# Scale and shift of a modulated norm as columns on transposed rows, and a pool of their own for the head norms

## The chip, the cores and the metric

The kernel runs on one core of one Trainium2 chip. The metric is the device time of one execution in microseconds (us); several runs of each kernel are taken on the same chip, and their medians are compared. A core has five engines that work side by side, each through a queue of its own in a fixed order: PE (TensorE, the matrix multiplier; PEld is its weight load), DVE (VectorE), ACT (ScalarE), POOL (GpSimd) and SP (SyncE, which here issues the DMA transfers).

## The reference

The program runs two transformer blocks over 512 tokens of width 2048. The first block (sparse attention and a state-space mixer) ends in a projection and a layernorm. The second block is a modulated one; this is its beginning, where the change sits:

```python
def rms_norm(x, g):
    xf = x.astype(jnp.float32)
    y = xf * lax.rsqrt(jnp.mean(xf * xf, axis=-1, keepdims=True) + EPS)
    return (y * g.astype(jnp.float32)).astype(x.dtype)
...
        sub = jnp.einsum('bse,ed->bsd', mixed, w_out[layer])
        h = _layer_norm(DEEPNORM_ALPHA * h + sub, ln_g[layer], ln_b[layer])
...
    mod_shared = jax.nn.silu(c) @ w_mod + b_mod
        mod = (mod_shared + mod_layer[l])[:, None, :]
        shift1, scale1, gate1, shift2, scale2, gate2 = jnp.split(mod, N_MOD, axis=-1)
        h = rms_norm(x, norm1_g[l]) * (1.0 + scale1) + shift1
        proj = h @ w_in[l]
        u_a, v_a, q, k, v = jnp.split(proj, SPLIT_POINTS, axis=-1)
        y_a = chunked_spatial_gating(u_a, v_a, gm_norm_g[l], gm_ws[l], gm_bs[l])
        q = rms_norm(q.reshape(B, S, N_SB_HEADS, HEAD_DIM), q_norm_g[l])
        k = rms_norm(k.reshape(B, S, N_SB_HEADS, HEAD_DIM), k_norm_g[l])
```

Behind it come stick-breaking attention, an output projection, a second modulated norm and a mixture of 32 experts of which each token uses two.

## The kernel before, in words

The 512 tokens lie in four tiles of 128, called rows 0 to 3 here (one token on each partition, 2048 values along it). For a matmul the rows must be transposed, so that the 2048 features stand on partitions, 16 blocks of 128.

All large products are exact to fp32 by splitting: each operand becomes a high part, cast to the matmul's fp32r type on ACT (L123, `split_into`), and a low part, the rest, subtracted on DVE (L124); `mm3` (L148 to L150) multiplies high by high, high by low and low by high. Weights stream in chunks: SP loads 512 KB into `raw` (4 buffers, L136), ACT casts it into `wh`, DVE subtracts `wl` (3 buffers each), PE multiplies. With two rows of tokens a chunk is 12 matmuls of 128x512.

`phase_b` computes the w_out product for rows 0 and 1, then for rows 2 and 3, in 4 column blocks of 8 chunks each. Behind each block DVE adds the residual (L761) and gathers statistics (L762); behind each pair of rows `norms` runs for each of the two. It applies the layernorm (L780, L781, into `r`), stores the row (L782), squares it on ACT (L783), gets the reciprocal root from small DVE operations (L192 to L197), and then for each quarter of 512 features multiplies on DVE (L788) and adds on GpSimd (L789):

```python
            nc.vector.scalar_tensor_tensor(t[:, c], r[:, i, c], rs, g1[:, c], OP.mult, OP.mult)
            nc.gpsimd.tensor_tensor(t[:, c], t[:, c], s1[:, c], OP.add)
            self.rows_to_op(t[:, c], self.opt[2 * b:2 * b + 2], i)
```

`rows_to_op` transposes four blocks into a PSUM tile `s` on PE (L203) and splits them into `op` from there (L123, L124). Here g1 is norm1_g times (1 + scale1) and s1 is shift1, each one value for a feature, so each is loaded broadcast over all 128 partitions: 128x2048, 1 MB. `load(k)` spreads these loads over the first blocks.

`mixer2` then multiplies the normed rows by w_in: q for rows 0 and 1, k for rows 0 and 1, q for rows 2 and 3, k for rows 2 and 3, 8 chunks each. Each result gets a norm by heads of 128 (`head_norm`: four squares on ACT at L798, DVE's reciprocal root, L803 writes `row`), four transposes of `row` and a copy (L835).

The order on each engine is fixed when the program is built: a scheduler places the instructions of all engines by modelled times and data dependences, so code that is written later can stand between earlier code's instructions, and matmuls of q's and k's chunks between transposes. Tiles come from pools; a pool on the right side of the memory (`side='right'`) lies where an earlier one lay, and its tiles wait for the old tiles' last readers. `ln` holds lng, lnb, g1, s1 and the work tiles of the norm; `b2`, with gq, gk, go, gm, ws and the head norms' tiles, comes after it in the same place. `issue_after` asks the scheduler to put an instruction behind a named one.

Of the kernel before, what the change touches and what calls it, by code (L numbers as in the profile page):

```python
# [12 lines left out]
F32 = mybir.dt.float32  # L13
# [3 lines left out]
AF = mybir.ActivationFunctionType  # L17
OP = mybir.AluOpType
# [5 lines left out]
KT = 16  # L24
# [79 lines left out]
class Kern:  # L104
# [622 lines left out]
    def phase_b(self):  # L727
        tc, nc, a = self.tc, self.nc, self.a
        kw = dict(bufs=1, side='right', reuse_waits='tile')
        r = self.r = self.rr.tile([128, 4, 2048], F32, name='r')  # L730
        self.x1 = self.dram.tile([512, 2048], F32, name='x1')
        with tc.tile_pool(name='ln', **kw) as ln:
            t = [ln.tile([128, 2048], F32, name=n) for n in ('lng', 'lnb', 'g1', 's1')]
            lng, lnb, g1, s1 = t
            st = ln.tile([128, 4, 4, 6], F32, name='st')

            def load(k):

# [12 lines left out]

            for half in ((0, 1), (2, 3)):
                for b in range(4):
                    ps = self.gemm('R', a['w_out'][b], self.opm, bg=1, toks=half)
                    if half[0] == 0:
                        with tc.issue_after(self.last_load.ins):
                            load(2 * b)
                            load(2 * b + 1)
                    for i in half:
                        c = slice(b * 512, b * 512 + 512)  # L760
                        nc.vector.scalar_tensor_tensor(r[:, i, c], r[:, i, c], ALPHA, ps[i], OP.mult, OP.add)  # L761
                        nc.vector.bn_stats(st[:, i, b, :], r[:, i, c])  # L762
                for i in half:
                    self.norms(ln, i, st[:, i], lng, lnb, g1, s1)
        with tc.tile_pool(name='rt', **kw) as self.rt:
            with tc.tile_pool(name='b2', **kw) as b2:
                self.mixer2(b2, self.opt)
            with tc.tile_pool(name='m0', **kw) as self.m0:
                self.route()

    def norms(self, ln, i, st, lng, lnb, g1, s1):

        nc, r = self.nc, self.r
        mv = ln.tile([128, 2], F32, tag='mv', name='mv', bufs=2)
        nc.vector.bn_aggr(mv, st.rearrange('p b s -> p (b s)'))
        nc.vector.tensor_scalar(mv[:, 1:2], mv[:, 1:2], 1e-5, None, OP.add)
        rs = self.rsqrt(mv[:, 1:2], 1)
        t = ln.tile([128, 2048], F32, tag='t', name='t', bufs=2)
        ss = ln.tile([128, 4], F32, tag='ss', name='ss', bufs=2)
        nc.vector.scalar_tensor_tensor(t, r[:, i, :], mv[:, 0:1], lng, OP.subtract, OP.mult)  # L780
        nc.vector.scalar_tensor_tensor(r[:, i, :], t, rs, lnb, OP.mult, OP.add)  # L781
        nc.sync.dma_start(self.x1[i * 128:(i + 1) * 128, :], r[:, i, :])  # L782
        nc.scalar.activation(t, r[:, i, :], AF.Square, accum_out=ss[:, 0:1])  # L783
        nc.vector.tensor_scalar(ss[:, 0:1], ss[:, 0:1], 1.0 / 2048, 1e-6, OP.mult, OP.add)
        rs = self.rsqrt(ss[:, 0:1], 1)
        for b in range(4):
            c = slice(b * 512, b * 512 + 512)
            nc.vector.scalar_tensor_tensor(t[:, c], r[:, i, c], rs, g1[:, c], OP.mult, OP.mult)  # L788
            nc.gpsimd.tensor_tensor(t[:, c], t[:, c], s1[:, c], OP.add)  # L789
            self.rows_to_op(t[:, c], self.opt[2 * b:2 * b + 2], i)  # L790

    def head_norm(self, pool, x, g, out, scale=1.0 / 128, eps=1e-6):

        nc = self.nc
# [5 lines left out]
        rs = self.rsqrt(ss, 4)  # L800
        for h in range(4):
            c = slice(h * 128, h * 128 + 128)
            nc.vector.scalar_tensor_tensor(out[:, c], x[:, c], rs[:, h:h + 1], g[h], OP.mult, OP.mult)  # L803

    def mixer2(self, b2, op):
        tc, nc, a, r = self.tc, self.nc, self.a, self.r
        kw = dict(bufs=1, side='right', reuse_waits='tile')
        gq = self.row_bcast(b2, a['q_norm_g'], 128, 'gq')
        gk = self.row_bcast(b2, a['k_norm_g'], 128, 'gk')
        bs = b2.tile([128, 4], F32, name='bs')  # L810
        nc.sync.dma_start(bs, a['gm_bs'])
        one = b2.tile([128, 128], F32R, name='one')
# [13 lines left out]
        with tc.tile_pool(name='sb', **kw) as sb:  # L826
            for b, g, half in ((0, gq, (0, 1)), (1, gk, (0, 1)), (0, gq, (2, 3)), (1, gk, (2, 3))):
                ps = self.gemm('R', a['w_in_2'][b], op, bg=1, toks=half)
                xT = qk[b]
                for i in half:  # L830
                    t = b2.tile([128, 512], F32, tag='row', name='row', bufs=3)
                    self.head_norm(b2, ps[i], [g] * 4, t)
                    pt = self.sps()
                    self.transposes(pt, [t[:, h * 128:(h + 1) * 128] for h in range(4)])
                    nc.scalar.copy(xT[:, :, i * 128:(i + 1) * 128], pt.rearrange('p (h t) -> p h t', h=4))  # L835
# [15 lines left out]
            for b in range(4):  # L851
                nc.sync.dma_start(self.gate1[b], self.mod[:, 4096 + b * 512:4608 + b * 512].broadcast_to([128, 512]))

            nc.vector.tensor_tensor(ws, ws, self.mask_le[:, None, :].to_broadcast([128, 4, 128]), OP.mult)
            ps = self.gemm('R', a['w_in_2'][3], op)
            for i in range(4):
                t = b2.tile([128, 512], F32, tag='row', name='row', bufs=3)
                vn = b2.tile([128, 512], F32, tag='row', name='vn', bufs=3)
                nc.scalar.activation(t, ps[i], AF.Gelu)
                self.head_norm(b2, t, [gm[:, h * 128:(h + 1) * 128] for h in range(4)], vn)  # L860
# [8 lines left out]
            ps.update(self.gemm('R', a['w_in_2'][4], op, toks=(2, 3)))  # L869
            opy = [self.op_tiles(c) for c in range(4)]  # L870
            for i in range(4):
                t = b2.tile([128, 512], F32, tag='row', name='row', bufs=3)
                self.head_norm(b2, o[:, i, :], [go[:, 512 + h * 128:512 + (h + 1) * 128] for h in range(4)], t)
                self.rows_to_op(t, opy[0:2], i)
            for i in range(4):
                t = b2.tile([128, 512], F32, tag='row', name='row', bufs=3)
                vn = b2.tile([128, 512], F32, tag='row', name='vn', bufs=3)
                nc.scalar.activation(t, ps[i], AF.Gelu)  # L878
                nc.vector.tensor_tensor(t, t, sg[:, i, :], OP.mult)
                self.head_norm(b2, t, [go[:, h * 128:(h + 1) * 128] for h in range(4)], vn)  # L880
                self.rows_to_op(vn, opy[2:4], i)
        self.opy = opy

# [568 lines left out]
```

## Time and profile before

| | before |
|---|---|
| median of 3 runs | 2021.39 us (2020.11 to 2024.66) |
| the profiled execution | 2020.36 us, its span 2018.5 us |
| mean granted TensorE clock | 0.973 of full speed |
| PE / DVE / ACT / POOL busy | 95% / 60% / 43% / 16% of the span |
| DMA | 502.85 MB, mean 249 GB/s |

The span is the time from the first to the last instruction in the profile of one execution; the 1.9 us beside it are start and end of the program. Busy shares are means over stages of very different character, so a single stage has to be read from the time windows. An instruction's waiting time is shown in brackets with what released it.

### The profile page before, as it was taken

The numbers are of one execution on the slowest core, as the hardware profiler recorded it, in microseconds if no ns is written. First come the engines' busy times: TensorE is split into PE (matmuls) and PEld (weight loads), VectorE is DVE, ScalarE is ACT, GpSimd is POOL, SyncE is SP. The second block draws the span as 40 slices with busy tenths as digits, with TensorE's granted clock in tenths as the row PEclk, the third lists the DMA queues.
The fourth block names the chain that finished last, engine by engine and source line by source line (L and its number), as shares of the span: only waits on it lengthen the run. The fifth ranks groups of instructions, "written<-read, shape, count | busy, mean of one in ns | idle before, by whom it ended". The sixth has DMA issues, their size and how long they took to land. (4 is left out here: it accounts for less than half of the span.)

```text
span 2018.5 us, 30419 instructions
## 1 busy us (share of the span) xinstructions
PE 1909.2 (95%) x11830; PEld 1232.9 (61%) x11830; DVE 1217.5 (60%) x2210; ACT 862.8 (43%) x1426; POOL 325.9 (16%) x251
## 2 busy tenths in 40 slices
PE   8999999999999999999997999889589999999996
PEld 5677776666777778887876888778442333333331
DVE  4778975444677796558796664877633434333433
ACT  3343223335443453434444554644234444444453
POOL 0422133000011110001111120043331111111111
PEclk9999999999999999999998999989699999999998
DMA  8654664545665674586654332656699999999994
GB/s 305 224 188 166 232 230 169 181 179 204 239 218 199 213 258 136 183 311 235 197 200 144 116 116 96 248 199 219 260 346 358 399 400 399 401 403 396 401 416 183
DMA packets 115493, 502.85 MB, mean 249 GB/s; under 512 B 22299, under 2 KB 23835, under 8 KB 84499
## 3 DMA queue, kind: packets, MB, share of 16 engines
q1 hardware_dynamic: 108642, 479.81, 64.0%
q0 software_dynamic: 6080, 16.83, 3.2%
q10 hardware_dynamic: 624, 4.24, 0.5%
q8 instruction: 94, 1.54, 0.3%
q14 instruction: 53, 0.43, 0.1%
HBM read 479.76 MB, written 37.84 MB: 256 GB/s over the span
## 5 line engine op out<-in xcount | busy, mean ns | idle before, releaser
L124 DVE TENSOR_TENSOR wl<-raw,wh 128x1024 fp32r<-128x1024 f32 (+1 forms) x272 | 357.8, 1320 | 224.4 <-ACT wh L123 223.5
L123 ACT CAST wh<-raw 128x1024 fp32r<-128x1024 f32 (+1 forms) x272 | 280.5, 1031 | 445.9 <-PE g L150 200.7
L149 PE MATMUL g<-wl,op 128*128 128x512 f32 (+1 forms) x896 | 351.0, 392 | 5.6 <-DVE wl L124 5.5
L150 PE MATMUL g<-wh,op 128*128 128x512 f32 (+1 forms) x896 | 348.3, 389 | 0.0
L148 PE MATMUL g<-wh,op 128*128 128x512 f32 (+1 forms) x896 | 333.7, 393 | 2.1 <-ACT row L878 1.0
L148 PE MATMUL g<-op,wh 128*128 128x512 f32 x672 | 272.0, 406 | 4.4 <-ACT z L404 3.0
L149 PE MATMUL g<-op,wh 128*128 128x512 f32 x672 | 268.1, 400 | 0.0
L150 PE MATMUL g<-op,wl 128*128 128x512 f32 x672 | 262.2, 396 | 0.0
L1178 PE MATMUL s<-wop,x 128*32 128x512 f32 x1710 | 251.4, 593 | 0.0
L1180 PE MATMUL s<-wop,x 128*32 128x512 f32 x570 | 251.0, 593 | 0.0
L148 PEld LDWEIGHTS g<-wh,op 128*128 128x128 f32 x896 | 171.2, 191 | 42.8 <-issue 6.6
L149 PEld LDWEIGHTS g<-wl,op 128*128 128x128 f32 x896 | 171.0, 191 | 41.6 <-DVE wl L124 8.5
L150 PEld LDWEIGHTS g<-wh,op 128*128 128x128 f32 x896 | 170.8, 191 | 33.4 <-issue 1.1
L1178 PEld LDWEIGHTS s<-wop,x 128*32 128x32 f32 x1710 | 68.2, 110 | 158.2 <-issue 154.0
L148 PEld LDWEIGHTS g<-op,wh 128*128 128x128 f32 x672 | 127.6, 190 | 52.9 <-issue 19.7
L150 PEld LDWEIGHTS g<-op,wl 128*128 128x128 f32 x672 | 127.3, 189 | 31.6 <-issue 3.9
L1188 ACT COPY yt<-g 32x512 f32<-32x512 f32 x192 | 111.3, 580 | 79.4 <-DVE y L1271 43.2
L149 PEld LDWEIGHTS g<-op,wh 128*128 128x128 f32 x672 | 127.9, 190 | 26.2 <-issue 1.4
L1178 PE MATMUL g<-wop,hT 128*32 128x512 f32 x810 | 120.7, 592 | 3.7 <-ACT hT L1227 2.2
L1189 DVE TENSOR_TENSOR gu<-gu,s 96x512 f32<-96x512 f32 x32 | 21.8, 682 | 169.5 <-ACT gu L1188 169.5
L1188 ACT COPY gu<-s 32x512 f32<-32x512 f32 x96 | 55.6, 579 | 159.1 <-PE s L1180 157.5
L1180 PE MATMUL g<-wop,hT 128*32 128x512 f32 x270 | 120.9, 594 | 0.0
(400 smaller groups left out, 2817.9 us busy)
## 6 DMA issues: line engine op xcount, KB each, us to landing
wop<-in_w_gu SPq DMA_DIRECT2D x95, 1024.0 KB
raw<-in_w_in SPq DMA_DIRECT2D x168, 512.0 KB
wm<-in_w_mod SPq DMA_DIRECT2D x96, 512.0 KB
raw<-in_w_mod SPq DMA_DIRECT2D x96, 512.0 KB
raw<-in_w_out SPq DMA_DIRECT2D x96, 512.0 KB
wop<-in_w_dn SPq DMA_DIRECT2D x45, 1024.0 KB
w<-in_w_gu SPq DMA_DIRECT2D x33, 1024.0 KB
w<-in_w_dn SPq DMA_DIRECT2D x19, 1024.0 KB
```

The lines of the kernel that those rows point to most:

```text
L123: nc.scalar.copy(hi, src)
L124: (lo_eng or nc.vector).tensor_tensor(lo, src, hi.bitcast(F32), OP.subtract)
L148: nc.tensor.matmul(out, lhsT=a[0], rhs=b[0], start=start, stop=False)
L149: nc.tensor.matmul(out, lhsT=a[0], rhs=b[1], start=False, stop=False)
L150: nc.tensor.matmul(out, lhsT=a[1], rhs=b[0], start=False, stop=stop)
L1178: nc.tensor.matmul(main[i][32 * s:32 * s + 32], lhsT=xs[i][:, 32 * s:32 * s + 32], rhs=w[i], start=first[i], stop=last[i], tile_position=( ...
L1180: self.mm = nc.tensor.matmul(ps[o][96:128], lhsT=xs[3][:, 32 * o:32 * o + 32], rhs=w[3], start=first[3], stop=last[3], tile_position=(0, 96))
L1188: self.last_copy = nc.scalar.copy(t[32 * s:32 * s + 32], ps[s][96:128])
L1189: nc.vector.tensor_tensor(t, t, main[0:W], OP.add)
```

## The change

The scale g1 and the shift s1 of the norm are no longer rows broadcast over partitions, but columns: one tile `n1col` of 128 partitions x 3 x 16, in which feature 128 k + p stands at partition p, place k. After the transposition a feature is a partition, so ACT can apply scale and shift as one value for each partition. Per row and quarter ACT now scales `r` by the token's reciprocal root (Copy with scale, 128x512), PE transposes, and ACT writes scale x value + shift for each of the four blocks (128x128) from PSUM into `f` in SBUF, from which `op` is split. The DVE multiplication and the GpSimd addition are gone. A pool `hn`, opened ahead of `ln` and not over its space, takes gq, gk and the tiles of all head norms (`row`, `vn`, hn_ss, hn_jk). The product of ws with its mask is placed behind the last head norm of q and k.

```diff
+        hn_cm = tc.tile_pool(name='hn', bufs=1)
+        self.hn = hn_cm.__enter__()
         with tc.tile_pool(name='ln', **kw) as ln:
-            t = [ln.tile([128, 2048], F32, name=n) for n in ('lng', 'lnb', 'g1', 's1')]
-            lng, lnb, g1, s1 = t
+            lng, lnb = [ln.tile([128, 2048], F32, name=n) for n in ('lng', 'lnb')]
             st = ln.tile([128, 4, 4, 6], F32, name='st')
+
+            col = ln.tile([128, 3, KT], F32, name='n1col')
...
-                elif k < 6:
-                    src = (a['norm1_g'], self.mod[:, 2048:4096], a['ln_g'], a['ln_b'])[k - 2]
-                    nc.sync.dma_start((g1, s1, lng, lnb)[k - 2], src.broadcast_to([128, 2048]))
+                elif k < 5:
+                    src = (a['norm1_g'], self.mod[:, 2048:4096], self.mod[:, 0:2048])[k - 2]
+                    nc.sync.dma_start(col[:, k - 2, :], src.rearrange('o (k p) -> p (o k)', p=128))
                     if k == 3:
-                        nc.vector.scalar_tensor_tensor(g1, s1, 1.0, g1, OP.add, OP.mult)
-                elif k == 6:
-                    nc.sync.dma_start(s1, self.mod[:, 0:2048].broadcast_to([128, 2048]))
+                        nc.vector.scalar_tensor_tensor(col[:, 0, :], col[:, 1, :], 1.0, col[:, 0, :], OP.add, OP.mult)
+                elif k < 7:
+                    nc.sync.dma_start((lng, lnb)[k - 5], (a['ln_g'], a['ln_b'])[k - 5].broadcast_to([128, 2048]))
...
-            nc.vector.scalar_tensor_tensor(t[:, c], r[:, i, c], rs, g1[:, c], OP.mult, OP.mult)
-            nc.gpsimd.tensor_tensor(t[:, c], t[:, c], s1[:, c], OP.add)
-            self.rows_to_op(t[:, c], self.opt[2 * b:2 * b + 2], i)
+            nc.scalar.activation(t[:, c], r[:, i, c], AF.Copy, scale=rs)
+            pt = self.sps()
+            self.transposes(pt, [t[:, (4 * b + j) * 128:(4 * b + j + 1) * 128] for j in range(4)])
+            f = ln.tile([128, 512], F32, tag='f', name='f', bufs=2)
+            for j in range(4):
+                k, cj = 4 * b + j, slice(j * 128, j * 128 + 128)
+                nc.scalar.activation(f[:, cj], pt[:, cj], AF.Identity, scale=g1[:, k:k + 1], bias=s1[:, k:k + 1])
+            for u in range(2):
+                o, ts = self.opt[2 * b + u], slice(i * 128, i * 128 + 128)
+                self.split_into(o[0][:, :, ts], o[1][:, :, ts], f[:, u * 256:(u + 1) * 256].rearrange('p (k t) -> p k t', k=2))
...
-        gq = self.row_bcast(b2, a['q_norm_g'], 128, 'gq')
-        gk = self.row_bcast(b2, a['k_norm_g'], 128, 'gk')
+        gq = self.row_bcast(self.hn, a['q_norm_g'], 128, 'gq')
+        gk = self.row_bcast(self.hn, a['k_norm_g'], 128, 'gk')
...
-                    t = b2.tile([128, 512], F32, tag='row', name='row', bufs=3)
-                    self.head_norm(b2, ps[i], [g] * 4, t)
+                    t = self.hn.tile([128, 512], F32, tag='row', name='row', bufs=3)
+                    self.head_norm(self.hn, ps[i], [g] * 4, t)
...
-            nc.vector.tensor_tensor(ws, ws, self.mask_le[:, None, :].to_broadcast([128, 4, 128]), OP.mult)
+            with tc.issue_after(self.last_hn.ins):
+                nc.vector.tensor_tensor(ws, ws, self.mask_le[:, None, :].to_broadcast([128, 4, 128]), OP.mult)
```

The scheduler moves the instructions around these lines. PE, where the chunks of q and k for rows 0 and 1 meet the transposes of rows 2 and 3 (`t` is the normed row, `row` a head norm's output, `cst` the identity). Before:

```order
L150 MATMUL g<-wh,op 128x512
L148 MATMUL g<-wh,op 128x512
L149 MATMUL g<-wl,op 128x512
L150 MATMUL g<-wh,op 128x512
L203 MATMUL s<-cst,t 128x128 x16
L203 MATMUL s<-cst,row 128x128 x4
L148 MATMUL g<-wh,op 128x512
L149 MATMUL g<-wl,op 128x512
L150 MATMUL g<-wh,op 128x512
```

After, the transposes of row 3:

```order
L203 MATMUL s<-cst,t 128x128 x8
...
L150 MATMUL g<-wh,op 128x512
L203 MATMUL s<-cst,t 128x128 x4
...
L150 MATMUL g<-wh,op 128x512
L203 MATMUL s<-cst,t 128x128 x4
L148 MATMUL g<-wh,op 128x512
...
L150 MATMUL g<-wh,op 128x512
L203 MATMUL s<-cst,row 128x128 x4
```

Before, the sixteen transposes and the first of `row` stood in one piece behind a chunk; after, they stand in packs of eight, four and four with a chunk between them, and the first transposes of `row` follow half a chunk later.

ACT from the last Square of the norm (row 3) on. Before:

```order
L783 ACTIVATE t,ss<-r 128x2048
L123 CAST op<-s 128x2x128 x2
L123 CAST wh<-raw 128x1024
L123 CAST op<-s 128x2x128 x4
L123 CAST wh<-raw 128x1024 x5
L123 CAST op<-s 128x2x128 x4
L798 ACTIVATE hn_jk,hn_ss<-g 128x128 x3
```

After (the Square is at L787, the column operation at L798, the scaled copy at L792, the head norm's square at L809):

```order
L787 ACTIVATE t,ss<-r 128x2048
L809 ACTIVATE hn_jk,hn_ss<-g 128x128
L798 ACTIVATE f<-s,n1col 128x128 x8
L123 CAST wh<-raw 128x1024
L123 CAST op<-f 128x2x128 x3
L792 ACTIVATE t<-r,rs_y 128x512 x4
L123 CAST op<-f 128x2x128
L123 CAST wh<-raw 128x1024
L798 ACTIVATE f<-s,n1col 128x128 x4
L123 CAST wh<-raw 128x1024
L798 ACTIVATE f<-s,n1col 128x128 x4
L123 CAST wh<-raw 128x1024
```

Up to the cast of the chunk that starts at 1090.83 in the trace of before, the queue of after holds behind that Square 32 column operations, 7 casts of wh, 12 of op, 4 scaled copies, 6 head-norm squares and 2 copies of transposed rows.

SP's loads ahead of the mixer. Before:

```order
L136 DMA raw<-in_w_in 128x1024 x8
L712 DMA gq<-in_q_norm_g 128x128
L712 DMA gk<-in_k_norm_g 128x128
L811 DMA bs<-in_gm_bs 128x4
L712 DMA go<-in_out_norm_g 128x1024
L712 DMA gm<-in_gm_norm_g 128x512
L825 DMA ws<-in_gm_ws 128x512
```

After:

```order
L136 DMA raw<-in_w_out 128x1024 x7
L712 DMA gq<-in_q_norm_g 128x128
L712 DMA gk<-in_k_norm_g 128x128
L136 DMA raw<-in_w_out 128x1024
L743 DMA r<-in_x 128x2048 x2
L136 DMA raw<-in_w_out 128x1024 x8
L746 DMA n1col<-in_norm_g 128x16x1
L746 DMA n1col<-mod 128x16x1
L136 DMA raw<-in_w_out 128x1024 x8
L746 DMA n1col<-mod 128x16x1
```

The loads of gq and gk moved from the q and k chunks to the first w_out chunks, where the three column loads now stand too; bs, go, gm and ws stay among the chunks of w_in.

## Rows read from the trace of the kernel before

**Rows 1.** The page, part 1: busy time, share of the span and instructions.

```profile
PE 1909.2 (95%) x11830; PEld 1232.9 (61%) x11830; DVE 1217.5 (60%) x2210; ACT 862.8 (43%) x1426; POOL 325.9 (16%) x251
```

**Rows 2.** Windows: start:end, length, busy us of each engine, granted clock, DMA share, GB/s.

```profile
840.00:937.34 97.34, 97.34 (x431) 80.30 (x430) 63.29 (x73) 39.24 (x38) 0.00 (x0) 1.00 0.78 292
937.34:1090.83 153.49, 133.86 (x598) 109.01 (x597) 128.16 (x265) 67.57 (x117) 31.13 (x16) 0.93 0.55 179
979.83:1009.79 29.96, 29.96 (x134) 24.77 (x132) 18.73 (x25) 13.23 (x17) 0.00 (x0) 1.00 0.65 208
1042.70:1049.50 6.80, 6.41 (x17) 4.88 (x18) 5.13 (x9) 2.57 (x5) 0.33 (x1) 0.50 0.97 329
1090.83:1127.16 36.33, 36.33 (x165) 30.03 (x164) 21.56 (x46) 18.37 (x37) 0.00 (x0) 1.00 0.61 202
```

**Rows 3.** Groups of ACT by shape, 937.34 to 1090.83: busy, mean ns, idle before.

```profile
L123 ACT CAST wh<-raw 128x1024 fp32r<-128x1024 f32 x43 | 45.3, 1054 | 62.8 <-PE g L150 59.5 <-issue 2.4 <-ACT op L123 0.6
L123 ACT CAST op<-s 128x256 fp32r<-128x256 f32 x32 | 10.6, 376 | 7.4 <-DVE op L124 5.8 <-PE s L203 1.5
```

**Rows 4.** L203 from `t`, all in the trace: count, lowest/mean/highest ns.

```profile
L203 PE MATMUL s<-cst,t x64: 270/272/473, 951.4 to 1066.0; 128*128 128x128 f32 x64
```

**Rows 5.** Timeline of PE: start, us, instruction, idle before and its releaser.

```profile
955.15 0.66 PE L203 MATMUL s<-cst,t 128*128 128x128 f32 x4 [2.28 <-POOL t L789]
...
1038.06 0.62 PE L148 MATMUL g<-wh,op 128*128 128x512 f32 x2
...
1062.71 1.47 PE L203 MATMUL s<-cst,t 128*128 128x128 f32 x12
...
1078.09 1.16 PE L203 MATMUL s<-cst,row 128*128 128x128 f32 x4 [11.81 <-DVE row L803]
```

**Rows 6.** PE's waits, 937 to 1091: total us, times, longest.

```profile
PE s L203 <- DVE row L803: 11.8, 1, 11.8
PE s L203 <- POOL t L789: 6.6, 4, 2.6
```

**Rows 7.** Timeline of SP: start, us of issue, transfer.

```profile
1067.06 0.42 SPq L712 DMA_DIRECT2D gq<-in_q_norm_g  x1
...
1072.11 5.49 SPq L890 DMA_DIRECT2D col<-mod  x1
```

**Rows 8.** Timeline of POOL, the last row's additions.

```profile
1058.32 7.25 POOL L789 TENSOR_TENSOR t<-t,s 128x512 f32<-128x512 f32 x4 [15.29 <-DVE t L788]
```

**Rows 9.** Timeline of DVE.

```profile
1023.01 1.23 DVE L124 TENSOR_TENSOR wl<-raw,wh 128x1024 fp32r<-128x1024 f32 x1 [0.40 <-ACT wh L123]
...
1024.74 2.35 DVE L781 SCALAR_TENSOR_TENSOR r<-t,rs_y,lnb 128x2048 f32<-128x2048 f32 x1
...
1076.59 0.69 DVE L854 TENSOR_TENSOR ws<-ws,cst 128x512 f32<-128x512 f32 x1 [4.06 <-DMA ws<-in_gm_ws]
```

**Rows 10.** Timeline of ACT.

```profile
955.92 1.17 ACT L123 CAST op<-s 128x256 fp32r<-128x256 f32 x4
...
1035.54 1.06 ACT L123 CAST wh<-raw 128x1024 fp32r<-128x1024 f32 x1 [1.21 <-PE g L150]
...
1042.00 1.91 ACT L783 ACTIVATE t<-r 128x2048 f32<-128x2048 f32 x1 [2.04 <-DVE r L781]
...
1380.90 2.56 ACT L986 ACTIVATE h<-h,rs_y 128x512 f32<-128x512 f32 x4 [2.17 <-DVE rs_y L197]
```

**Rows 11.** Groups of ACT by shape, whole span: busy, mean ns, idle before.

```profile
L530 ACT ACTIVATE cacc<-cu,vec_a 128x512 f32<-128x512 f32 x16 | 13.1, 816 | 0.4
L696 ACT ACTIVATE p<-p,mx 128x512 f32<-128x512 f32 x8 | 5.8, 723 | 2.5 <-DVE mx L695 2.4
L696 ACT ACTIVATE p<-p,mx 128x128 f32<-128x128 f32 x8 | 3.2, 402 | 8.0 <-DVE mx L695 8.0
```

**Rows 12.** ACT's waits, 840 to 940: total us, times, longest.

```profile
ACT wh L123 <- DMA raw<-in_w_out: 9.2, 4, 4.1
```

**Rows 13.** PE's waits, 1285 to 1370.

```profile
PE s L203 <- DVE vn L803: 8.2, 3, 3.3
```

More of the change, by code (lines that the diff above doesn't have):

```diff
@@ L763, in phase_b @@
                 for i in half:
-                    self.norms(ln, i, st[:, i], lng, lnb, g1, s1)
+                    self.norms(ln, i, st[:, i], lng, lnb, col[:, 0, :], col[:, 2, :])
         with tc.tile_pool(name='rt', **kw) as self.rt:
@@ L767, in phase_b @@
                 self.mixer2(b2, self.opt)
+            hn_cm.__exit__(None, None, None)
             with tc.tile_pool(name='m0', **kw) as self.m0:
@@ L802, in head_norm @@
             c = slice(h * 128, h * 128 + 128)
-            nc.vector.scalar_tensor_tensor(out[:, c], x[:, c], rs[:, h:h + 1], g[h], OP.mult, OP.mult)
+            self.last_hn = nc.vector.scalar_tensor_tensor(out[:, c], x[:, c], rs[:, h:h + 1], g[h], OP.mult, OP.mult)
     def mixer2(self, b2, op):
@@ L852, in mixer2 @@
                 nc.sync.dma_start(self.gate1[b], self.mod[:, 4096 + b * 512:4608 + b * 512].broadcast_to([128, 512]))
-            nc.vector.tensor_tensor(ws, ws, self.mask_le[:, None, :].to_broadcast([128, 4, 128]), OP.mult)
+            with tc.issue_after(self.last_hn.ins):
+                nc.vector.tensor_tensor(ws, ws, self.mask_le[:, None, :].to_broadcast([128, 4, 128]), OP.mult)
             ps = self.gemm('R', a['w_in_2'][3], op)
             for i in range(4):
-                t = b2.tile([128, 512], F32, tag='row', name='row', bufs=3)
-                vn = b2.tile([128, 512], F32, tag='row', name='vn', bufs=3)
+                t = self.hn.tile([128, 512], F32, tag='row', name='row', bufs=3)
+                vn = self.hn.tile([128, 512], F32, tag='row', name='vn', bufs=3)
                 nc.scalar.activation(t, ps[i], AF.Gelu)
-                self.head_norm(b2, t, [gm[:, h * 128:(h + 1) * 128] for h in range(4)], vn)
+                self.head_norm(self.hn, t, [gm[:, h * 128:(h + 1) * 128] for h in range(4)], vn)
                 pt = self.sps()
@@ L871, in mixer2 @@
             for i in range(4):
-                t = b2.tile([128, 512], F32, tag='row', name='row', bufs=3)
-                self.head_norm(b2, o[:, i, :], [go[:, 512 + h * 128:512 + (h + 1) * 128] for h in range(4)], t)
+                t = self.hn.tile([128, 512], F32, tag='row', name='row', bufs=3)
+                self.head_norm(self.hn, o[:, i, :], [go[:, 512 + h * 128:512 + (h + 1) * 128] for h in range(4)], t)
                 self.rows_to_op(t, opy[0:2], i)
             for i in range(4):
-                t = b2.tile([128, 512], F32, tag='row', name='row', bufs=3)
-                vn = b2.tile([128, 512], F32, tag='row', name='vn', bufs=3)
+                t = self.hn.tile([128, 512], F32, tag='row', name='row', bufs=3)
+                vn = self.hn.tile([128, 512], F32, tag='row', name='vn', bufs=3)
                 nc.scalar.activation(t, ps[i], AF.Gelu)
                 nc.vector.tensor_tensor(t, t, sg[:, i, :], OP.mult)
-                self.head_norm(b2, t, [go[:, h * 128:(h + 1) * 128] for h in range(4)], vn)
+                self.head_norm(self.hn, t, [go[:, h * 128:(h + 1) * 128] for h in range(4)], vn)
                 self.rows_to_op(vn, opy[2:4], i)
```

## The prediction

> **What bounds the kernel now.** I read the engine shares first: PE is busy 95% of the span [rows 1], so only time in which PE stands still, or runs at half clock, can be won. The stretches show where that is [rows 2]. From 1090.83 to 1127.16 PE is busy without a gap at full clock; what arrives earlier at 1090.83 therefore ends earlier, one for one. The stretch ahead, 937.34 to 1090.83, is where the change sits: 153.49 us long, PE busy 133.86 of them, mean clock 0.93. It holds the second half of the w_out gemm, the norms of all four rows of tokens and the first q and k chunks.
>
> How much of it is lost? A weight chunk is 12 matmuls and one cast of wh on ACT. From 979.83 to 1009.79 PE never stops, at full clock, and runs 134 matmuls, 11 chunks and an edge [rows 2]: 29.96 / 11 = 2.72 us for a chunk. The stretch has 43 casts, thus 43 chunks [rows 3]. It has 80 transposes too (64 of the norm, 16 of head-norm rows), each (1.47 − 0.27) / 11 = 0.11 us apart, 12 taking 1.47 and one alone 0.27 [rows 4, 5]. Unstalled: 43 × 2.72 + 80 × 0.11 = 125.8 us. So 153.5 − 125.8 = **27.7 us are lost**.
>
> The waits of PE name 18.4 of them [rows 6]: 11.8 in one wait for `row`, the head norm's output (L803), and 6.6 in four for `t`, GpSimd's shift (L789). The other 9.3 lie in short waits and above all in half-clock work: in 1042.70 to 1049.50 PE is busy 6.41 us at granted clock 0.50, which is 3.2 us of work at the full level (2.4 GHz) [rows 2], and it follows the longest wait for `t`, 2.6.
>
> Why is `row` late? Follow it back. The load of gq is issued only at 1067.06 [rows 7], since its tile lies over one that GpSimd's last L789 reads, and L789 of the last row runs to 1065.6 [rows 8]. Behind gq come go, gm and ws in SP's queue; the mask product of ws (L854) stands in DVE's queue ahead of the head norm and waits 4.06 us for its load [rows 9]. Only then do L803 and, at 1078.09, PE's transposes go [rows 5].
>
> **The change, part by part.**
>
> Removed: 16 L788 on DVE and 16 L789 on GpSimd. The latter set when `t` is ready (6.6 us of PE), and their end released gq.
>
> Head-norm pool and order of loads: gq and gk are now issued behind the seventh w_out load, ahead of the whole stretch, and nothing of ln's space holds them. ws's mask product goes behind the last head norm. Both causes of the 11.8 wait are gone; what is late next is ACT.
>
> Added on ACT: per row 4 scaled copies (128x512) and 16 column operations (128x128). The copy has a row: 4 of L986 take 2.56 us, 0.64 each, about 0.62 apart [rows 10]. The column form with two pointers is not in the trace. A 128x128 operation with one pointer lasts 402 ns; the second pointer costs 816 − 723 = 93 ns at 128x512 [rows 11]; so 0.495 us alone. In a queue instructions overlap: a cast of op lasts 0.376 alone [rows 3], four in a row 1.17 [rows 10], thus (1.17 − 0.376) / 3 = 0.265 apart, 0.70 of it. By that share 0.495 becomes 0.35. I take **0.40**, between 0.35 and 0.495 and nearer the packed end, as the order puts them in packs of 4 to 8. ACT's extra work: 16 × 0.62 + 64 × 0.40 = 35.5 us. In the stretch ACT is busy only 67.57 of 153.49 us [rows 2], so most hides; whether all does is decided behind the Square of the last row.
>
> Rows 0 and 1 (up to 1010): transposes now stand between chunks that are ready, so the wait of 2.28 for `t` at 955.15 [rows 5] goes, with some 0.9 of short waits and half clock around it: **3.2**, bounds 1.6 (f at 0.495 instead) and 4.7 (all that is lost ahead of 1038).
>
> Rows 2 and 3, in the times of before. PE starts a chunk at 1038.06 [rows 5], and nine chunks on it stands at 1090.83: 52.8 us for 9 × 2.72 + 48 × 0.11 = 29.8, so 23.0 of the 27.7 are lost here. In the changed order ACT sets the pace. The wh cast at 1035.54 [rows 10] ends at 1036.6, DVE's wl takes 1.23, then the last layernorm product (2.35) [rows 9]: the Square of row 3 starts at 1040.2. From there to the cast of the chunk of 1090.83, ACT has in its queue: 1 Square 1.9 [rows 10], 32 column operations 12.8, 7 wh casts 7.0 (1.05 alone), 12 op casts 3.2, 4 copies of t 2.5, 6 head-norm squares 2.4 (as 128x128 operations at 0.40) and 2 copies of transposed rows 1.2 (as copies of t): 31.0 us, so 1071.2; with wl 1072.4. PE's own work from 1038.06, 9 × 2.72 + 44 × 0.11 (one pack of four stands later now) is done at 1067.4, and four waits that the walk through the two orders gives on the way (wl 0.5, op 0.35 and 0.7, row 0.9) make it 1069.9. So PE waits another 2.5 for the cast. Loss left 2.5 + 2.5 = 5.0, won 23.0 − 5.0 = **18.0**. With f at 0.35 ACT is 1.6 earlier, at 0.495 3.0 later.
>
> DVE: it loses those 16 and the 128x2048 product that made g1, and gets one of 128x16; its queue is lighter, counted at nothing, since behind the Square the wl that PE needs follows a late cast, not a late DVE. GpSimd gets nothing.
>
> Loads: 3 of 1 MB become 3 of 2048 four-byte elements. A load of this form holds SP's issue 5.49 us at L890 [rows 7]. I take **0**: they are issued among the first w_out loads, where ACT already waits 9.2 us for raw, up to 4.1 at once [rows 12], and PE is busy 97.34 of 97.34 us [rows 2]; the removed 3 MB free the same queue. Bound above: 3 × 5.49 = 16.5 us, if the four raw buffers are empty each time. bs, go, gm, ws and the router's columns come in the middle of the k chunks; raw for the chunk of 1090.83 is then still ahead of its cast.
>
> Sum: 3.2 + 18.0 = 21.2. I take off 1.2 for hand-overs between ACT, PE and DVE that such a walk leaves out: **20 us**. The profiled run has 2020.36 us around its span of 2018.5, 1.0 under the median 2021.39: 2020.36 − 20 + 1.0 = **2001**.
>
> **Rivals.**
> - *ACT is the harder bound.* f costs 0.495 and the waits it makes throw PE to the lower clock level twice, as the wait for `t` did (3.2 each): 20 − 3.0 − 1.6 − 2 × 3.2 = 9.0, so 2012; with one such stretch 2009. For it: ACT's 31.0 us are dense. Against: the waits in the walk are under 2.5 us.
> - *Column loads starve the weights*: 2001 to 2017.5. For it: 5.49 us of issue for 8 KB. Against: raw's four buffers and the freed megabytes.
> - *The tail gives it back.* Later head norms (vn, 8.2 us of PE waits in 1285 to 1370 [rows 13]) are in a slightly different order; ±3 us, and 2009 if these waits double.
> - *Not faster: ACT's added work lands on PE.* Place: behind the Squares, where wh casts queue behind column operations. If all 35.5 us were in series with PE: 2021.4 − 27.7 + 35.5 = 2029. It decides from the point where over 27.7 of 35.5 us reach PE; the same cause between 20 and 27.7 would be no change. Against: ACT stands idle 86 us of the stretch, and in rows 0 and 1 the column operations fall between casts of chunks that are three buffers ahead. The Trainium skill ("ScalarE: Activation LUTs", Rules for kernel authors) speaks against the change: multiplies and adds belong on VectorE, per element up to about 3 times faster in bf16. By that factor the 35.5 us would be an estimated 12 on VectorE, and the sum would go towards this rival's 2029; no run here shows a VectorE form of this column operation, and the data is fp32.
>
> **How the numbers follow.** Forecast 0.73 (its own range 1996 to 2006: f at 0.35, no hand-overs and all of rows 0 and 1 add 1.6 + 1.2 + 1.5 to the 20, so 1997; f at 0.495 takes off 4.6, so 2006). ACT harder 0.14, loads 0.04, tail 0.03, ACT on PE 0.06 (0.03 of it without a measurable loss). A difference under 0.2%, 4 us, is about what a measurement here cannot tell from none. Faster 0.89, same 0.05, slower 0.06. Range 1994 to 2011: below, all 27.7 lost us come back (2020.4 − 27.7 + 1 = 1993.7); above, the harder ACT with its first stretch.
>
> **What would show it.** In the changed profile: no wait of PE for `row` over 2 us; gq's load far ahead; POOL idle in the stretch; ACT busy about 100 us of some 133; the stretch from the chunk of 937.34 to that of 1090.83 at 133 ± 4 us; the column operations 0.3 to 0.5 us. The prediction is wrong if PE waits several us each for `f`, `op` or wh (ACT bound), if ACT waits for raw with PE behind it (loads), or if the time behind 1127 does not shift as a block.

## The result and the profile after

The changed kernel took 1993.97 us (median of 6 runs, 1986.69 to 2002.75), the kernel before 2020.86 beside it (6 runs, 2015.47 to 2024.72). The medians are 26.9 us apart; the recorded ratio is 0.9878, 95% interval 0.9855 to 0.9901: about 24.7 us less, with an interval of 20 to 29. Forecast were 20 us (2001, range 1994 to 2011). Direction and place were right; the gain was some 5 us larger than the sum, and the median stands at the lower edge of the range.

The profiled execution after is one of the long ones, 2002.75 us with a span of 2000.9, so its total shows only 17.6 us. It came to the stretch of the change late: the first chunk, at 937.34 before, starts at 944.86. Of these 7.5 us, 5.6 are there already ahead of every changed load (the 113th subtraction of wl on DVE starts at 818.48 before and at 824.08 after), so most of the lateness does not come from the change. I therefore measure from that chunk to the one that starts at 1127.16 before, where PE has been saturated for a while. The windows of the kernel before and after (columns as in [rows 2]), before first:

```profile
937.34:1127.16 189.82, 170.19 (x761) 139.04 (x760) 149.72 (x310) 85.94 (x153) 31.13 (x16) 0.95 0.56 183
1127.16:1290.00 162.84, 162.84 (x831) 136.30 (x830) 103.62 (x284) 87.54 (x193) 19.76 (x33) 1.00 0.34 117
```

```profile
944.86:1111.52 166.66, 163.73 (x761) 134.76 (x760) 124.99 (x293) 115.25 (x233) 0.00 (x0) 1.00 0.64 208
944.86:1013.84 68.98, 68.98 (x322) 57.32 (x320) 48.57 (x88) 47.09 (x82) 0.00 (x0) 1.00 0.62 209
1013.84:1075.82 61.98, 60.37 (x286) 49.36 (x285) 52.73 (x141) 49.81 (x113) 0.00 (x0) 1.00 0.56 195
1045.00:1075.00 30.00, 29.13 (x143) 23.66 (x142) 23.50 (x82) 30.00 (x79) 0.00 (x0) 1.00 0.45 152
1111.52:1274.30 162.78, 162.78 (x830) 136.14 (x829) 104.34 (x285) 87.46 (x193) 19.64 (x33) 1.00 0.34 118
```

The same 761 recorded matmuls take 189.82 us before and 166.66 after: **23.2 us less**. PE's idle time (length less busy) falls from 19.6 to 2.9 us, and its busy time from 170.19 to 163.73: that second part, 6.5 us, is work that no longer runs at half clock (mean granted clock 0.95 before, 1.00 after). The next 162.8 us are equal to 0.1, so the lead is passed on whole. Unstalled, by the prediction's estimate, the stretch would take 125.8 us and the 36.33 of the saturated piece [rows 2], 162.1 in all: 4.5 us are still lost.

The waits of PE in that stretch after, where [rows 6] stood before (total, times, longest):

```profile
PE g L149 <- DVE wl L124: 2.6, 3, 1.3
PE g L148 <- ACT wh L123: 0.3, 1, 0.3
```

No wait for `t` or `row` is left. ACT's two new operations, grouped over the same stretch:

```profile
L798 ACT ACTIVATE f<-s,n1col 128x128 f32<-128x128 f32 x64 | 24.9, 519 | 0.0
L792 ACT ACTIVATE t<-r,rs_y 128x512 f32<-128x512 f32 x16 | 10.5, 737 | 0.0
```

Three places of ACT's timeline: the last Square, the first pack of column operations behind it, and the cast for the chunk that starts at 1090.83 before:

```profile
1043.65 1.92 ACT L787 ACTIVATE t<-r 128x2048 f32<-128x2048 f32 x1
...
1045.81 2.90 ACT L798 ACTIVATE f<-s,n1col 128x128 f32<-128x128 f32 x8
...
1070.81 1.29 ACT L123 CAST wh<-raw 128x1024 fp32r<-128x1024 f32 x1
```

The two are 35.4 us busy together on ACT, which has not an idle moment from 1045 to 1075. PE's longest wait in the stretch, 1.3 us, is not ACT's doing: DVE's product of the router's columns (L904) waits 5.65 us for its load, and wl stands behind it, in DVE's timeline:

```profile
1090.45 0.17 DVE L904 SCALAR_TENSOR_TENSOR col<-col 128x16 f32<-128x16 f32 x1 [5.65 <-DMA col<-mod]
1090.56 1.22 DVE L124 TENSOR_TENSOR wl<-raw,wh 128x1024 fp32r<-128x1024 f32 x1
```

### The profile page after: what moved, and what is told of

Read it like the earlier page. It is cut to its first block, busy times and chain, and to the rows that moved or that the text cites. A ratio compares the mean times of both kernels' runs of the same rounds, so it can differ in the third digit from the quotient of the medians.

```text
span 2000.9 us, 30444 instructions
## 1 busy us (share of the span) xinstructions
PE 1903.2 (95%) x11830; PEld 1226.3 (61%) x11830; DVE 1192.6 (60%) x2194; ACT 891.3 (45%) x1506; POOL 293.7 (15%) x235
## 5 line engine op out<-in xcount | busy, mean ns | idle before, releaser
L124 DVE TENSOR_TENSOR wl<-raw,wh 128x1024 fp32r<-128x1024 f32 (+1 forms) x272 | 351.0, 1294 | 214.2 <-ACT wh L123 205.2
L1201 DVE TENSOR_TENSOR gu<-gu,s 96x512 f32<-96x512 f32 x32 | 21.8, 682 | 170.3 <-ACT gu L1200 170.3
```

What stands on the lines that cost most here:

```text
L124: (lo_eng or nc.vector).tensor_tensor(lo, src, hi.bitcast(F32), OP.subtract)
L1201: nc.vector.tensor_tensor(t, t, main[0:W], OP.add)
```

## The experiments

The theory: two causes that have little to do with each other, `t` late because of GpSimd and `row` late because of gq and the mask product, each with half-clock work behind it. The rivals: one cause alone (GpSimd's late end) explains both; ACT or the column loads set what is left. In each trace the stretch runs from the same chunk to the same chunk, all windows with the columns of [rows 2].

### The kernel before once more, and the changed one

> The kernel before once more, for a second profile of it. The stretch from the chunk of 937.34 to that of 1127.16 took 189.8 us in the first. If my reading of the gain holds (it is made in the stretch and not by chance), it is 187 to 191 again, while its start may lie some us elsewhere, as the stages ahead differ from run to run (768 to 780 us at the same weight chunk in eight profiles so far).

> The changed kernel once more, for a second profile. In the first one it came to the stretch 7.5 us later than the kernel before, and its runs lie 16 us apart. If that is chance of the stages ahead, the stretch takes 130.3 +-1 us again (43 chunks from the same chunk) while the time to its start differs by several us; if the change itself makes the loads ahead late, the start is again 5 to 8 us later than in the kernel before.

```profile
943.96:1132.40 188.44, 169.21 (x762) 138.55 (x761) 149.91 (x310) 86.01 (x153) 31.18 (x16) 0.95 0.58 185
```

```profile
943.22:1109.03 165.81, 163.90 (x761) 134.69 (x760) 125.03 (x293) 114.95 (x233) 0.00 (x0) 1.00 0.66 209
```

The first is the kernel before, the second the changed one. The stretch repeats, 189.82 and 188.44 against 166.66 and 165.81, while its start does not: 937.34 and 943.96 for the kernel before, 944.86 and 943.22 for the changed one. The lateness of the first profile was mostly chance of the stages ahead; 1 to 2 us of it lie among the changed loads (below). The 43 chunks to the chunk of 1090.83 before take 127.3 us in both profiles of the changed kernel; the 130.3 of the expectation reaches into the 44th, which ends at 131.0 and 130.9. The new runs gave 1993.71 us (4 runs), ratio 0.9880 (0.9846 to 0.9914).

### One half of the change at a time

Columns only: gq, gk and the head norms' tiles go back to the pool over ln's space, the mask product to its old place.

```diff
-        gq = self.row_bcast(self.hn, a['q_norm_g'], 128, 'gq')
+        gq = self.row_bcast(b2, a['q_norm_g'], 128, 'gq')
...
-                    t = self.hn.tile([128, 512], F32, tag='row', name='row', bufs=3)
+                    t = b2.tile([128, 512], F32, tag='row', name='row', bufs=3)
...
-            with tc.issue_after(self.last_hn.ins):
-                nc.vector.tensor_tensor(ws, ws, self.mask_le[:, None, :].to_broadcast([128, 4, 128]), OP.mult)
+            nc.vector.tensor_tensor(ws, ws, self.mask_le[:, None, :].to_broadcast([128, 4, 128]), OP.mult)
```

> The column application alone; gq, gk and the head norms' tiles stay in the pool over ln's space and the mask product of ws where it was. Two separate causes (my theory): the waits for t and the half clock behind them go, but gq still waits for ln's last reader (now the last split of f) and the mask product still stands ahead of the first head norm, so PE keeps one wait of 5 to 12 us for row: the stretch of 43 chunks takes 141 to 147 us instead of 153.5, the whole 8 +-3 us less than before. Rival, one cause (GpSimd's late end alone): ln's space comes free early enough, no wait for row over 2 us, the stretch 130 to 134, about 20 us less.

Pool and mask product only: the kernel before with the pool `hn` and the later mask product; L788 and L789 stay.

```diff
-                    t = b2.tile([128, 512], F32, tag='row', name='row', bufs=3)
-                    self.head_norm(b2, ps[i], [g] * 4, t)
+                    t = self.hn.tile([128, 512], F32, tag='row', name='row', bufs=3)
+                    self.head_norm(self.hn, ps[i], [g] * 4, t)
...
```

> The pool for the head norms and the later mask product alone; scale and shift stay broadcast rows on DVE and GpSimd. Two causes: gq is there early, the wait of 11.8 for row goes, the four waits for t (6.6 us) and half clock behind them stay: the stretch 139 to 144 us, 12 +-3 us less than before. Rival, one cause: the op of the last row is as late as before (its last subtraction was at 1070.6), PE runs the head norms' transposes and then waits for op or t in row's place, 5 us or more: the stretch 147 to 153, under 6 us less.

The mask product alone: the kernel before with that one line moved.

```diff
-            nc.vector.tensor_tensor(ws, ws, self.mask_le[:, None, :].to_broadcast([128, 4, 128]), OP.mult)
+            with tc.issue_after(self.last_hn.ins):
+                nc.vector.tensor_tensor(ws, ws, self.mask_le[:, None, :].to_broadcast([128, 4, 128]), OP.mult)
```

> Only the mask product of ws goes behind the last head norm; all else as before. If the 4.06 us wait of that product in DVE's queue is part of the 11.8 us wait for row: the head norm starts when gq has landed, some 2 to 3 us behind its issue, so row is 4 to 6 us earlier and the stretch 148 to 150 us, 4 to 6 us less in all. If gq's own late load is all of it: the stretch within 1 us of 153.5, no change.

With columns only, the stretch and a piece of it:

```profile
944.49:1123.40 178.91, 165.62 (x761) 136.62 (x760) 125.66 (x294) 117.47 (x233) 0.00 (x0) 0.96 0.62 195
...
1066.10:1079.80 13.70, 5.37 (x15) 4.28 (x16) 8.65 (x53) 9.82 (x44) 0.00 (x0) 0.50 0.68 146
```

PE's long wait in it, and the load of gq in SP's timeline:

```profile
PE s L203 <- DVE row L811: 12.6, 1, 12.6
```

```profile
1065.45 0.43 SPq L712 DMA_DIRECT2D gq<-in_q_norm_g  x1
```

With pool and mask product only, the stretch, and PE's waits in it:

```profile
942.15:1125.69 183.54, 171.72 (x761) 139.46 (x760) 147.20 (x309) 86.40 (x153) 31.20 (x16) 0.96 0.60 189
```

```profile
PE s L203 <- POOL t L792: 5.9, 3, 2.6
PE g L149 <- DVE wl L124: 2.9, 5, 1.4
PE s L203 <- DVE row L806: 2.4, 1, 2.4
```

With the mask product alone, the same two views:

```profile
938.55:1125.66 187.11, 171.02 (x761) 138.96 (x760) 149.10 (x309) 85.96 (x153) 31.16 (x16) 0.95 0.58 186
```

```profile
PE s L203 <- DVE row L803: 7.9, 2, 7.1
PE s L203 <- POOL t L789: 6.6, 4, 2.6
```

Against the mean of the two profiles of before, 189.1, the columns alone take off 10.2 us, pool and mask product 5.6, the mask product alone 2.0; the runs say 0.9955 (0.9931 to 0.9978), 0.9975 (0.9955 to 0.9995) and 0.9985 (0.9968 to 1.0002). The whole change takes off 22.5 to 23.3. Counted as the expectations count, to the chunk of 1090.83 before, the three took 142.6, 145.0 and 150.8 us: the columns within the range of two causes, the other two between the ranges of the two readings.

Two causes are confirmed: each half removes its own wait, or most of it, and leaves the other's. With the columns alone PE waits 12.6 us for `row`, with 13.7 us at half clock around it. With the pool alone GpSimd's `t` still costs 5.9. The one-cause theory falls with the first: GpSimd does nothing there, and the wait for `row` is as long as before. Not separated is whether `t` is late by GpSimd's additions or by DVE's products ahead of them, for which GpSimd itself waits 15.29 us [rows 8].

My reading of why `row` is late was only half right. With the columns alone gq is loaded at 1065.45, and its load has landed by 1069.83 (the last update of its semaphore in the trace), 4.1 us before `row` is made. What comes last there is the head norm's own chain: its squares on ACT (into hn_jk) start at 1069.44, released, by the profile, by DVE's split of `f`, which reads ln's space, and `row` follows behind the reciprocal root, in DVE's timeline:

```profile
1071.04 0.17 DVE L807 TENSOR_SCALAR hn_ss<-hn_ss 128x4 f32<-128x4 f32 x1 [0.56 <-ACT hn_jk L806]
...
1073.93 1.12 DVE L811 SCALAR_TENSOR_TENSOR row<-g,rs_y,gq 128x128 f32<-128x128 f32 x4
```

In the kernel before, gq has landed by 1071.77, and `row` comes at 1077.59, behind the mask product that waited 4.06 us. So what the pool frees is above all the head norm's work tiles, which lay over ln's space like gq; no run moves gq or these tiles alone.

And my size for the pool, 12 us, is wrong; the rival's "under 6" hit it. The halves do not add: 10.2 + 5.6 = 15.8, and 7 us come only when both are there. The windows say where: 3.3 of them are idle time of PE and 3.8 busy time (by the means of the two profiles of before and of the changed kernel). The pool alone takes 7.4 to 7.8 us of idle time from PE (to 11.8), but PE's busy time grows by 1.5 to 2.5: its remaining waits still bring half-clock work. Only without either wait does the clock stay up (1.00, against 0.96 with either half and 0.95 before).

### What ACT has left

> The changed kernel with the 64 column operations as one DVE instruction each (multiply and add by two columns), nothing of them on ScalarE. If ScalarE's queue behind the last Square is what is left of the loss (it was busy 30 of 30 us from 1045 to 1075 in the changed profile), the chunk behind it starts up to 2 us earlier: stretch from the chunk of 937.34 to that of 1127.16 at 164 to 166 us. If ScalarE was hidden but for 0.9 us, the stretch stays 165.8 to 166.7 or grows, since DVE gets the work (estimate 64 x 0.2 to 0.4 = 13 to 26 us, and it is the engine that makes wl and op). By the Trainium skill's rule for adds and multiplies the DVE form should be the shorter one: under the 0.497 us of ScalarE.

```diff
-                nc.scalar.activation(f[:, cj], pt[:, cj], AF.Identity, scale=g1[:, k:k + 1], bias=s1[:, k:k + 1])
+                nc.vector.tensor_scalar(f[:, cj], pt[:, cj], g1[:, k:k + 1], s1[:, k:k + 1], OP.mult, OP.add)
```

> The changed kernel with each of the 64 column operations done twice into the same place: 64 x 0.35 = 22 us more on ScalarE, half of it behind each pair of rows. If ScalarE is the engine that ends last behind the last Square (busy 30 of 30 us), the 11 us of rows 2 and 3 reach PE but for a few: stretch 173 to 178 us, row waits or wh waits of PE. If it still has room, the stretch stays under 169. For rows 0 and 1 (to the chunk of 1018) no change is expected: 74.2 +-1 us.

```diff
+                nc.scalar.activation(f[:, cj], pt[:, cj], AF.Identity, scale=g1[:, k:k + 1], bias=s1[:, k:k + 1])
                 nc.scalar.activation(f[:, cj], pt[:, cj], AF.Identity, scale=g1[:, k:k + 1], bias=s1[:, k:k + 1])
```

With the column operations on DVE, the stretch, PE's longest waits, the operation's own line (lowest, median, highest ns) and a pack of eight of it in DVE's timeline:

```profile
942.99:1115.85 172.86, 165.44 (x761) 136.50 (x760) 141.24 (x357) 97.22 (x169) 0.00 (x0) 0.98 0.63 201
```

```profile
PE s L203 <- DVE row L814: 4.7, 1, 4.7
PE s L203 <- ACT t L792: 2.0, 1, 2.0
```

```profile
L798 DVE TENSOR_SCALAR f<-s,n1col x64: 393/400/410, 957.7 to 1069.3; 128x128 f32<-128x128 f32 x64
```

```profile
1061.63 2.63 DVE L798 TENSOR_SCALAR f<-s,n1col 128x128 f32<-128x128 f32 x8
```

With each done twice on ACT, the stretch and PE's longest waits:

```profile
943.77:1116.49 172.72, 165.90 (x761) 136.29 (x760) 126.83 (x293) 136.71 (x297) 0.00 (x0) 0.98 0.63 199
```

```profile
PE s L203 <- ACT f L799: 3.4, 2, 2.6
PE g L148 <- ACT op L123: 1.7, 1, 1.7
```

On DVE the operation is shorter (400 ns against a median of 497 on ACT; in a pack they are closer, (2.63 − 0.40) / 7 = 0.32 us apart against 0.34), and the stretch is 6 to 7 us longer: 172.86, runs 0.9911 (0.988 to 0.9941). DVE also makes wl, op and `row`; it is busy 141 of 173 us, and PE waits for `row` again. On ACT 22 us more work cost 6 to 7 us of the stretch (172.72, runs 0.9899, 0.9875 to 0.9922), all of it behind rows 0 and 1: the first 24 chunks take 68.93 us, against 68.98. The expectation of 173 to 178 was a little high; ACT has room for part of the 11 us behind rows 2 and 3, not for all. So of the two engines tried ACT is the cheaper place for this work, and it is close to full.

### The mask product with the rest of the change

> The changed kernel without the line that puts the mask product of ws behind the last head norm. It then stands in DVE's queue ahead of the second k head norm, in front of the wait for the router's columns. ws is issued at 1078.5 in the changed profile and that head norm runs near 1080: a wait of 1 to 4 us in DVE, of which PE feels 0 to 2. My theory: stretch 166 to 168.5. Rival (the line carries part of the gain, as it did alone, 2.7 us): stretch 169 or more.

```diff
-            with tc.issue_after(self.last_hn.ins):
-                nc.vector.tensor_tensor(ws, ws, self.mask_le[:, None, :].to_broadcast([128, 4, 128]), OP.mult)
+            nc.vector.tensor_tensor(ws, ws, self.mask_le[:, None, :].to_broadcast([128, 4, 128]), OP.mult)
```

The stretch, and DVE's waits for loads in it:

```profile
943.83:1109.50 165.67, 163.78 (x761) 134.75 (x760) 125.61 (x294) 115.05 (x233) 0.00 (x0) 1.00 0.64 209
```

```profile
DVE col L903 <- DMA col<-mod: 2.1, 1, 2.1
DVE ws L865 <- DMA ws<-in_gm_ws: 1.9, 1, 1.9
```

165.67 us, as with the line; runs 1991.71, ratio 0.9871 (0.9838 to 0.9904). Once the head norms have their own pool, this line is worth nothing that these runs can tell: the 1.9 us wait for ws only takes the place of a part of the router columns' wait.

### The column loads

> The changed kernel with each of the three column loads issued three times (the first two into tiles that nothing reads). If they are hidden behind the w_out gemm, as forecast: the time from the last chunk ahead of them to the chunk of 937.34 and the total do not change (within 1 us), only ScalarE's waits for raw grow. If they starve the weights: 6 more loads, up to 4 to 5.5 us of issue each, make the start of the stretch up to 20 us later.

```diff
...
+                    nc.sync.dma_start(sp[:, k - 2, :], src.rearrange('o (k p) -> p (o k)', p=128))
+                    nc.sync.dma_start(sp2[:, k - 2, :], src.rearrange('o (k p) -> p (o k)', p=128))
                     nc.sync.dma_start(col[:, k - 2, :], src.rearrange('o (k p) -> p (o k)', p=128))
```

> The changed kernel with its three column loads issued by GpSimd instead of SP. Tripling them cost 6 us between the weight chunk ahead of them and the stretch (117.4 to 123.6 us), about 1 us for each load; so the three themselves should cost 1 to 3 us through SP. If SP's issue is what costs: 115.5 to 116.5 us there, and 1 to 3 us less in all. If the transfers of 2048 elements of 4 bytes themselves take the weights' place in the DMA engines: 117 to 118 as before.

```diff
-                    nc.sync.dma_start(col[:, k - 2, :], src.rearrange('o (k p) -> p (o k)', p=128))
+                    nc.gpsimd.dma_start(col[:, k - 2, :], src.rearrange('o (k p) -> p (o k)', p=128))
```

ACT's waits for raw from 840 to 960 in three kernels: the changed one, with tripled loads, with the loads issued by GpSimd.

```profile
ACT wh L123 <- DMA raw<-in_w_out: 10.4, 5, 5.1
```

```profile
ACT wh L123 <- DMA raw<-in_w_out: 20.3, 8, 6.1
```

```profile
ACT wh L123 <- DMA raw<-in_w_out: 5.1, 3, 4.7
```

With GpSimd the loads moved in time too: they are out at 788 to 792, while SP issues them at 862 to 884 in the changed kernel. From POOL's timeline:

```profile
788.18 1.42 POOL L746 DMA_DIRECT2D n1col<-in_norm_g  x1
789.60 2.35 POOL L746 DMA_DIRECT2D n1col<-mod  x2
```

The time from the 113th subtraction of wl on DVE (818.48 in the first profile of before, and ahead of all changed loads but these by GpSimd) to the 153rd (934.25) shows what PE's weights feel:

| kernels | 113th to 153rd wl, us |
|---|---|
| no column loads, but 3 MB of broadcast rows: before, twice; pool only; mask product alone | 115.8, 115.7; 116.2; 116.9 |
| three column loads by SP: after, twice; columns only; mask product early; on DVE; doubled | 117.7, 117.1; 116.8; 116.2; 118.1; 118.1 |
| three by GpSimd, issued some 30 us ahead of the 113th | 116.1 |
| nine by SP | 123.6 |

Six loads more cost 123.6 − 117.3 = 6.3 us. What PE feels of that is above all one stop, and it comes by way of DVE: the product of the norm's columns stands in DVE's queue ahead of wl and waits for its load. DVE and PE in the changed kernel, then with tripled loads:

```profile
869.09 0.18 DVE L748 SCALAR_TENSOR_TENSOR n1col<-n1col 128x16 f32<-128x16 f32 x1 [5.47 <-DMA n1col<-mod]
...
870.48 0.50 PE L149 MATMUL g<-wl,op 128*128 128x512 f32 x1 [0.60 <-DVE wl L124]
```

```profile
880.10 0.18 DVE L752 SCALAR_TENSOR_TENSOR n1col<-n1col 128x16 f32<-128x16 f32 x1 [8.40 <-DMA n1col<-mod]
...
881.49 0.79 PE L149 MATMUL g<-wl,op 128*128 128x512 f32 x1 [3.53 <-DVE wl L124]
```

With tripled loads the granted clock from 880 to 890 is 0.66 on top. So 6.3 / 6, about 1 us a load, is a quotient and not the price of a load. The three of the change cost 117.3 − 116.2 = 1.2 by the means of the six profiles with them and the four without, which overlap by single values; seen directly is a wait of PE for wl of 0.5 to 0.6 us behind that product, in three of the six. The forecast of 0 was short by about that. Whether SP's issue or the transfers are the cost, the run with GpSimd cannot tell, since it also moved the loads to another place. Runs: tripled 0.9913 (0.9879 to 0.9948), by GpSimd 0.9876 (0.9849 to 0.9903), the latter not to be told from the changed kernel.

### The wait that is left, and a version with all of it

> The changed kernel with the router's three column loads and their product moved to the head norms' pool, so that they are issued among the first w_out loads. In the changed profile they hold SP from 1080 to 1089 and DVE waits 5.6 us for them with wl and a head norm behind; PE stands 1.3 us at 1090.5 and the lead over the kernel before shrinks from 17.7 to 15.6 us there. My theory: that wait is what is late next; without it the stretch takes 163.5 to 165 instead of 165.8 to 166.7 and the total 1 to 3 us less than the changed kernel. Rival: the lead shrinks by the other order of row's transposes alone; stretch as before, no difference.

```diff
+        col = self.col2 = self.hn.tile([128, 3, KT], F32, name='col')
+        nc.sync.dma_start(col[:, 0, :], a['norm2_g'].rearrange('o (k p) -> p (o k)', p=128))
...
-        col = xr.tile([128, 3, KT], F32, name='col')
+        col = self.col2
```

> The version that the runs so far point to: the changed kernel, the router's columns loaded early into the head norms' pool, and all six column loads issued by GpSimd. The early router columns alone took the stretch to 165.1 us but cost 4 us ahead of it. If SP's issue was that cost: 115.5 to 116.5 us ahead, the stretch 164.5 to 165.5, and 2 to 4 us less than the changed kernel in all, near 1990. If not: within 1 us of the changed kernel.

```diff
-        nc.sync.dma_start(col[:, 0, :], a['norm2_g'].rearrange('o (k p) -> p (o k)', p=128))
+        nc.gpsimd.dma_start(col[:, 0, :], a['norm2_g'].rearrange('o (k p) -> p (o k)', p=128))
...
```

The stretch, first with the router's columns early, then with all six loads by GpSimd:

```profile
941.56:1106.65 165.09, 163.50 (x761) 134.85 (x760) 125.22 (x292) 115.09 (x233) 0.00 (x0) 1.00 0.63 210
```

```profile
942.08:1107.23 165.15, 163.56 (x762) 134.87 (x761) 125.22 (x292) 115.14 (x233) 0.00 (x0) 1.00 0.63 210
```

Both take the wait of L904 away and the stretch to 165.1, of 165.2 to 166.7 in the five profiles with the same order of transposes and the wait: 0.1 to 1.6 us, less than expected. Both give it back ahead of the stretch (121.1 and 119.7 from the 113th to the 153rd wl). In the second GpSimd issues the norm's three at 787 to 791 and the router's three at 835 to 839, among the weights' loads, and these three cost 119.7 − 116.1 = 3.5 us, about as much as by SP (121.1 − 117.3 = 3.8); ACT's longest wait for raw there:

```profile
851.72 1.04 ACT L123 CAST wh<-raw 128x1024 fp32r<-128x1024 f32 x1 [7.70 <-DMA raw<-in_w_out]
```

So in that place, by one profile each, it is not SP's issue that costs, and the expected 115.5 to 116.5 was missed. Runs: 0.9897 (0.9868 to 0.9925) and 0.9868 (0.9845 to 0.9890; 1989.88 us, 6 runs). No version is told apart from the changed kernel.

## Why the prediction was right, and where its sum was off

**Place and mechanism.** The lost 27.7 us were there to be won, and what the trace named is what went: 11.8 for `row`, 6.6 for `t`, and the half-clock work behind them. One link of the walk back was wrong: gq's late load was not what `row` waited for last (above); the pool was the right remedy by its other tiles. Two profiles of each kernel agree on 22 to 24 us in the stretch (188.4 and 189.8 against 165.8 and 166.7).

**Rows 0 and 1, 3.2 forecast.** The chunk that starts at 1009.79 before starts at 1013.84 after, so the late start of 7.52 has shrunk to 4.05: 3.5 us won (4.5 against the second profile of before). Right.

**Rows 2 and 3, 18.0 forecast, then 1.2 off for hand-overs.** This is the mis-sized term. One chunk behind the walk's end, the chunk of 1093.55 starts at 1075.82, so 21.8 us are won from 1013.84 on. At the walk's own end, the chunk of 1090.83, PE starts at 1072.15: the 43 chunks took 127.3 us, below the 133 ± 4 that the prediction gave as a sign, and 0.9 us of waits follow inside that chunk. PE before, then after:

```profile
1093.55 0.61 PE L148 MATMUL g<-wh,op 128*128 128x512 f32 x2
```

```profile
1072.15 0.73 PE L148 MATMUL g<-wh,op 128*128 128x512 f32 x2 [0.35 <-ACT wh L123]
1073.41 0.50 PE L149 MATMUL g<-wl,op 128*128 128x512 f32 x1 [0.53 <-DVE wl L124]
```

The walk was right up to the last Square (forecast 1040.2 + 4.05 = 1044.25, measured 1043.65). From there to the end of the chunk's cast it gave 31.0 us, and it took 28.5 (1070.81 + 1.29 − 1043.65). The column operation lasts 497 ns, as bounded (495), but packs of eight run (2.90 − 0.50) / 7 = 0.34 apart, at the low end of the bounds and not at 0.40: 11.0 us for the 32, each counted to the start of the next, and not 12.8. The six head-norm squares took 1.6 and not 2.4. And the four waits of PE on the way, 2.5 us in the walk, did not appear. The 2.5 us wait for the cast came out as 0.35 for wh and 0.53 for wl. The deduction for hand-overs had nothing to stand for. Behind it, 2.1 us are given back up to 1111.52: 0.4 is the pack of transposes that stands later, 1.3 PE's wait for wl behind the router's columns, whose loads I named, but not the product in DVE's queue that waits for them.

**Loads, 0 forecast:** 1.2 us by the means, near what the profiles can tell. The term looked at raw alone; what reached PE came by DVE's product of the columns, which waits 5.47 us for its load ahead of wl.

**DVE's lighter queue, counted at nothing.** It is not nothing: filled again with column operations, the stretch grows by 6 to 7 us.

**The rivals.** ACT as the harder bound did not happen, but is near: 22 us more on it cost 6 to 7. Starved weights did in part, some 1.2 us of the bound of 16.5. The tail: from 1127.16 to the end before and after the same order of chunks takes 891.4 and 887.3 us in the two profiles of before and 878.6 to 889.4 in those with the change, a spread larger than any difference: no loss shows, the rest is left open. ACT on PE fell. The rule of the Trainium skill ("ScalarE: Activation LUTs", Rules for kernel authors), that multiplies and adds belong on VectorE, agrees for the single operation, by 400 against 497 ns; its factor of up to about 3 is for bf16, and in fp32 no run shows it. Followed here it costs 6 to 7 us, with VectorE the engine that PE then waits for.

## What to carry to other kernels

Two waits that each bring half-clock work have to be removed together: half of the change, taken alone, gave a quarter or not quite half of the gain. Put an elementwise step on the engine that ends first in that stretch, not on the one whose instruction is shortest, and look whose queue it stands in. And a tile that is needed early should not lie over space that the stage before still reads; here the small tiles of a head norm, with a mask product behind them, held the matrix engine for 11.8 us.

## What the runs showed of the hardware that I had not expected

A column operation of ACT with two pointer operands from PSUM (128x128, fp32) lasts 497 ns, and in a pack the operations start 0.34 us apart; the same on DVE lasts 400 ns, 0.32 apart. A load of 2048 elements of 4 bytes held SP for 0.4 to 6.8 us. The stages ahead of the change differ by up to 13 us between executions (767.3 to 780.5 us at the 105th wl over 14 profiles, in kernels whose code is the same up to there), which is most of why one profile's total could show 17.6 us for a gain of 23.
